# SiLU-gated product on one core: a 16-element transfer ahead of the first load, and a first store in one piece instead of three

## The chip, the core and the metric

The kernel runs on one core of a Trainium2 chip. Five engines of the core matter by name: ScalarE (ACT) and VectorE (DVE) compute, SyncE (SP) and ScalarE issue the DMA transfers, GpSimd (POOL) fills four constant tiles at the start; TensorE has no work. Sixteen DMA engines move the data between HBM and the on-chip memory SBUF, which has 128 partitions. Loads are issued by SyncE and go through DMA queue q1; stores are issued by ScalarE and go through q10. The metric is the device time of one execution in microseconds; smaller is better.

## The reference

The input has 32 x 512 = 16384 rows of 2048 float32. Each row is split in two halves of 1024; the output row is silu(first half) times second half.

```python
x = np.random.randn(32, 512, 2048).astype(np.float32)
half_dim = x.shape[-1] // 2
x1, x2 = x[..., :half_dim], x[..., half_dim:]
silu_x1 = x1 * (1 / (1 + np.exp(-x1)))
return (silu_x1 * x2).astype(np.float32)
```

So 134.22 MB are read and 67.11 MB written, and each element takes one activation or one multiply.

## The kernel before, in words

The rows are cut into 16 tiles of 1024 rows: 128 partitions with K = 8 rows each. Two tiles lie one after the other in each partition's share of memory (`view`, with RUN = 2). For each partition a load reads 8 x 2048 float32, 64 KB in one run, and a store writes 8 x 1024 float32, 32 KB in one run. There are two input buffers `xt` and two output buffers `ot`, used in turn.

For each tile, ACT applies Silu in place to the first half of `xt` (line 96), DVE multiplies it by the second half into `ot` (line 102), SyncE issues the load of the tile after the next into the buffer that has just been used up, and ACT's queue issues the store. Every transfer goes through `move` (line 77), so all of them have that line in the profile. SyncE's queue holds the sixteen loads alone; ACT's queue holds activations and stores in the order of the program, which is written out by hand (`manual_schedule`).

Tile 0 is computed in four chunks of 2 rows per partition (FIRST), tile 15 in chunks of 2, 3 and 3 rows (LAST); all others in one piece. Tile 15 is stored in three pieces too, each as soon as its chunk is multiplied. Tile 0 is stored, after its last chunk, in three pieces by partition (OPENING): partitions 0, 4, 8, ... (32 of them); partitions 2, 6, 10, ... (32); and the 64 odd ones. With 16 DMA engines these give 2, 2 and 4 partitions per engine.

Transfers take their completion semaphores from a set of eight, in turn, in the order in which they are recorded; `after` fixes that order between a tile's load and store, which of the two goes first changing every four tiles (`load_first`). `implied` declares waits that another wait already includes, and `settle_all_but` lets SyncE see all earlier transfers land before the last.

Of the kernel before, what the change touches and what calls it, by code (L numbers as in the profile page):

```python
# [1 line left out]

# [4 lines left out]


@with_exitstack
def kernel(  # L10
    ctx: ExitStack,
    tc: tile.TileContext,
    x: bass.AP,
    out: bass.AP,
):


    nc = tc.nc
    P = nc.NUM_PARTITIONS

    x_flat = x.flatten_outer_dims()
    out_flat = out.flatten_outer_dims()
    num_rows, in_cols = x_flat.shape
    half = in_cols // 2
    dt = x_flat.dtype

    K = 8
    FIRST = [2] * (K // 2)
    LAST = [2, 3, 3]
    OPENING = [  # L30
        (slice(0, None, 4), slice(None)),
        (slice(2, None, 4), slice(None)),
        (slice(1, None, 2), slice(None)),
    ]
    RUN = 2
    n_tiles = num_rows // (P * K)

    pool = ctx.enter_context(tc.tile_pool(name="pool", bufs=1))
    xts = [pool.tile([P, K, in_cols], dt, name=f"xt{b}") for b in range(2)]
    ots = [pool.tile([P, K, half], dt, name=f"ot{b}") for b in range(2)]  # L40

    def view(flat, i):
        return flat.rearrange("(g p t k) d -> g t p k d", p=P, t=RUN, k=K)[i // RUN, i % RUN]

    ctx.enter_context(tc.manual_schedule(engines={mybir.EngineType.Activation, mybir.EngineType.DVE}))

    sent = []
    loads, stores, silus, muls = {}, {}, {}, {}

    def implied(later, earlier, reason):  # L50
        for x in later:
            for y in earlier:
                tc.declare_no_dep(x, y, reason=reason)

    def earlier(done, i):
        return [ins for j in range(i % 2, i, 2) for ins in done[j]]

    def after(later, first):
        tc.add_manual_dep(
            later,  # L60
            first.name,
            mybir.DependencyInfo(mybir.DependencyClass.NoSync, mybir.DependencyReason.DATA),
            reason="order in which the transfers take their semaphores",
        )

    def settle_all_but(n, others):
        rest = nc.sync.nop(nofuse=True)
        for ins in sent[:-n] + others:
            tc.add_manual_dep(
                rest.ins,  # L70
                ins.name,
                mybir.DependencyInfo(mybir.DependencyClass.Sync, mybir.DependencyReason.DATA),
                reason="sync sees each earlier transfer land before the last ones",
            )

    def move(queue, out, in_):
        ins = queue.dma_start(out=out, in_=in_).ins  # L77
        sent.append(ins)
        return ins

    def load(i):
        loads[i] = [move(nc.sync, xts[i % 2][:], view(x_flat, i))]
        if i >= 2:
            implied(loads[i], earlier(loads, i), "the multiplies that this load awaits came after those loads")
            implied(loads[i], earlier(silus, i), "the multiplies that this load awaits came after those activations")

    def parts(sizes):
        assert sum(sizes) == K
        return [slice(sum(sizes[:n]), sum(sizes[:n + 1])) for n in range(len(sizes))]

    def compute(i, ot, chunks):
        xt = xts[i % 2]
        silus[i], muls[i] = [], []
        for ks in chunks:
            silus[i].append(
                nc.scalar.activation(  # L96
                    out=xt[:, ks, :half],
                    in_=xt[:, ks, :half],
                    func=mybir.ActivationFunctionType.Silu,
                ).ins  # L100
            )
            muls[i].append(nc.vector.tensor_mul(out=ot[:, ks], in0=xt[:, ks, :half], in1=xt[:, ks, half:]).ins)  # L102
        implied(muls[i], loads[i], "each multiply awaits an activation that came after the load")
        if i >= 2:
            implied(silus[i], earlier(silus, i), "the load that this activation awaits came after those activations")
            implied(silus[i], earlier(muls, i), "the load that this activation awaits came after those multiplies")
            implied(muls[i], earlier(muls, i), "the store that this multiply awaits came after those multiplies")

    def store(i, ot, pieces):
        ov = view(out_flat, i)  # L110
        stores[i] = [move(nc.scalar, ov[ps, ks], ot[ps, ks]) for ps, ks in pieces]

    ALL = slice(None)
    load(0)
    load(1)
    for i in range(n_tiles):
        ot = ots[i % 2]
        last = i == n_tiles - 1
        compute(i, ot, parts(FIRST if i == 0 else LAST if last else [K]))
        pieces = [(ALL, ALL)]  # L120
        if i == 0:
            pieces = OPENING
        elif last:
            pieces = [(ALL, ks) for ks in parts(LAST)]
        load_first = i // 4 % 2
        if load_first and i + 2 < n_tiles:
            load(i + 2)
        store(i, ot, pieces)
        if load_first and i + 2 < n_tiles:
            after(stores[i][0], loads[i + 2][0])  # L130
        if not load_first and i + 2 < n_tiles:
            load(i + 2)
            after(loads[i + 2][0], stores[i][-1])
    settle_all_but(1, muls[n_tiles - 1])


# [1 line left out]
_INS = ['x']  # L138
_OUTS = [((32, 512, 1024), 'float32')]


# [23 lines left out]
```

## Time and profile before

| | us |
|---|---|
| median of 3 runs (470.85 to 471.16) | 471.05 |
| span of the profiled execution | 469.2 |
| DVE busy | 139.5 |
| ACT busy | 114.2 |
| q1 (loads), share of 16 DMA engines' span | 66.4% |
| q10 (stores), share of 16 DMA engines' span | 33.2% |
| one silu of a whole tile, 128x8192 | 7.03 |
| one multiply of a whole tile, 128x8192 | 8.69 |

The span runs from the first to the last instruction of the profiled execution; the time of a run has some 1.9 us around it. A page's "busy" leaves out instructions that only issue a DMA; those stand in the timeline as SPq and ACTq, with the time that the issuing took. "To landing" is the time from the issue of a transfer to its completion, waiting in the queue included. The trace also keeps a record of every single DMA packet: queue, start, duration and bytes. Here a packet is one partition's run (64 KB of a load, 32 KB of a store, 8 or 12 KB of the last store's pieces) or the 4-byte update of a semaphore with which each DMA engine ends its share of a transfer. A record does not name its DMA engine, but a packet begins within a few ns of the end of the one before it on the same engine, so the sixteen sequences can be told apart by their phase.

### The profile page before, as it was taken

How to read it: one execution, taken by the hardware profiler on the slowest of the kernel's cores; microseconds unless marked ns; L12 is line 12 of the kernel's file. 1: busy time of each engine (PE TensorE's matmuls, PEld its weight loads, DVE VectorE, ACT ScalarE, POOL GpSimd, SP SyncE). 2: the span in 40 equal slices, each digit the busy share in tenths (PEclk: the TensorE clock that was granted, in tenths of full speed). 3: DMA queues.
4: the chain of work that ended last, by engine and by line, in shares of the span. 5: the costliest groups of instructions: out<-in, count | busy, mean ns of one | idle time of the engine just before them, and what ended most of it. 6: DMA issues, size and time to landing. Idle time of an engine off the chain costs nothing.

```text
span 469.2 us, 156 instructions
## 1 busy us (share of the span) xinstructions
DVE 139.5 (30%) x21; ACT 114.2 (24%) x22; POOL 0.2 (0%) x4
## 2 busy tenths in 40 slices
DVE  0070522407034070330704307042070520605152
ACT  1051405032050410504105050050501405014060
POOL 0000000000000000000000000000000000000000
DMA  8999999999999999999999999999999999999998
GB/s 358 447 447 374 475 402 433 416 492 402 411 439 486 408 402 447 475 419 402 444 439 458 402 436 413 492 402 416 433 486 408 402 447 475 419 402 444 450 402 358
DMA packets 4928, 201.33 MB, mean 429 GB/s; under 512 B 576, under 2 KB 576, under 8 KB 576
## 3 DMA queue, kind: packets, MB, share of 16 engines
q1 hardware_dynamic: 2304, 134.22, 66.4%
q10 hardware_dynamic: 2624, 67.11, 33.2%
HBM read 134.22 MB, written 67.11 MB: 429 GB/s over the span
## 4 chain that ended last, share of the span: by engine, by line
DMA 72%; DVE 14%; ACT 11%; DVEq 1%; issue 0%; SPq 0%
DMA xt<-in_x_dram 72%; DVE ot L102 14%; ACT xt L96 11%; DVEq L160 1%; SPq L77 0%
## 5 line engine op out<-in xcount | busy, mean ns | idle before, releaser
L102 DVE TENSOR_TENSOR ot<-xt 128x8192 f32<-128x8192 f32 (+2 forms) x21 | 139.5, 6659 | 320.8 <-ACT xt L96 320.8
L96 ACT ACTIVATE xt<-xt 128x8192 f32<-128x8192 f32 (+2 forms) x21 | 112.9, 5400 | 341.4 <-DMA xt<-in_x_dram 341.4
L96 ACT ACT_TABLE_LOAD x1 | 1.3, 1283 | 0.7 <-PEq L149 0.7
L149 POOL MEMSET const-bfloat16-1.0<- 128x1 bf16 x1 | 0.1, 102 | 0.0
L149 POOL MEMSET const-uint8-127<- 128x1 uint8 x1 | 0.1, 102 | 0.0
L149 POOL MEMSET const-float32-0.0<- 128x1 f32 x1 | 0.1, 99 | 0.2 <-issue 0.2
L149 POOL MEMSET const-float32-1.0<- 128x1 f32 x1 | 0.1, 99 | 0.0
## 6 DMA issues: line engine op xcount, KB each, us to landing
out_dram<-ot ACTq DMA_DIRECT2D x14, 4096.0 KB, 42.0
out_dram<-ot ACTq DMA_DIRECT2D x3, 1024.0 KB, 12.0
out_dram<-ot ACTq DMA_DIRECT2D x2, 1536.0 KB, 7.9
out_dram<-ot ACTq DMA_DIRECT2D x1, 2048.0 KB, 37.2
xt<-in_x_dram SPq DMA_DIRECT2D x16, 42.2
```

The source lines that it names most:

```text
L96: nc.scalar.activation(out=xt[:, ks, :half], in_=xt[:, ks, :half], func=mybir.ActivationFunctionType.Silu,).ins
L102: muls[i].append(nc.vector.tensor_mul(out=ot[:, ks], in0=xt[:, ks, :half], in1=xt[:, ks, half:]).ins)
L149: nc = _bacc.Bacc("TRN2", target_bir_lowering=False, num_devices=1)
L160: with _tile.TileContext(nc) as tc:
```

## The change

Ahead of load 0, SyncE issues a transfer that writes sixteen float32 zeros, from a constant tile that GpSimd fills at the start, to sixteen places in HBM: the first element of the last of the 8 rows of every eighth partition, in the output of tile 15. The store of tile 15 writes the right values there later. With sixteen elements on sixteen partitions, each DMA engine moves one. Load 0 comes after it in the order in which the transfers take their semaphores; it has no wait on it.

OPENING becomes one piece, so tile 0 is stored by one transfer of 128 partitions, like tiles 1 to 14.

```diff
     OPENING = [
-        (slice(0, None, 4), slice(None)),
-        (slice(2, None, 4), slice(None)),
-        (slice(1, None, 2), slice(None)),
+        (slice(None), slice(None)),
     ]
...
     ALL = slice(None)
+    with nc.allow_non_contiguous_dma(reason="one element on each DMA engine, ahead of the first load"):
+        first = move(nc.sync, view(out_flat, n_tiles - 1)[::8, K - 1, :1], nc.const_aps.tensor(0.0, [16, 1], dt))
     load(0)
+    after(loads[0][0], first)
     load(1)
```

## Prediction

> **What bounds the kernel now.** I read the busy time by slice first, then the DMA queues, the chain, the windows at both ends, and last the trace's single DMA packet records.
>
> From the page, the busy slices and the queues:
>
> ```profile
> DMA  8999999999999999999999999999999999999998
> DMA packets 4928, 201.33 MB, mean 429 GB/s; under 512 B 576, under 2 KB 576, under 8 KB 576
> q1 hardware_dynamic: 2304, 134.22, 66.4%
> q10 hardware_dynamic: 2624, 67.11, 33.2%
> ```
>
> q1 carries SyncE's loads, q10 ScalarE's stores. Together their packets fill 99.6% of 16 engines' span, so nothing that DVE or ACT does matters unless it leaves an engine without work. The waits say the same from the other side: ACT waits for loads and nothing else.
>
> ```profile
> ACT xt L96 <- DMA xt<-in_x_dram: 341.4, 16, 22.1
> DVE ot L102 <- ACT xt L96: 320.8, 17, 24.6
> ```
>
> The chain and the timeline, at both ends (start us, duration us, what):
>
> ```profile
> 0.73 0.37 SPq L77
> 1.10 0.05 issue
> 1.15 44.20 DMA xt<-in_x_dram
> ...
> 33.53 1.86 ACTq L77 DMA_DIRECT2D out_dram<-ot  x3
> ...
> 453.35 0.34 ACTq L77 DMA_DIRECT2D out_dram<-ot  x1
> ...
> 457.07 3.60 ACTq L77 DMA_DIRECT2D out_dram<-ot  x2
> ```
>
> The first load is issued at 0.73, and its first packet starts at 1.734. The last packet ends at 468.042, the span at 469.187.
>
> The packet records (start, duration, bytes, queue) show what is lost. A 64 KB load packet takes 2.418 us and a 32 KB store packet 1.213 on every engine; consecutive packets leave no gap. A tile has 8 of each per engine, about 29.0 us. Only two groups are longer. The 16 packets that open load 0 take 2.94 to 3.45, mean 3.187: 0.77 over. And the 16 load packets that start at 36.1 to 36.8, each just before its engine's first store packet, take 3.16 to 3.47, mean 3.283: 0.86 over. After that no load packet is over 2.425. One engine starts at 2.425, the other fifteen at 1.734 to 1.963; that engine is also last at the end, 468.042 against 467.849 for the next.
>
> This engine around load 1's end (starts in us; sem is the 9 ns completion packet):
>
> ```
> 36.794 load 7, 3.368 long | 40.158 store 1 | 41.368 load 8 | 43.782 store 2
> 44.991 load sem | 44.997 store sem (first opening store) | 45.003 load 1 | 47.417 store 3
> ... 54.664 store sem (second) ... 71.578 store sem (third) | 71.584 load sem
> ```
>
> Each engine takes one packet from one queue, then one from the other, and a completion packet uses a turn like a data packet. From 71.58 on a load and a store end in adjacent turns; at the end 448.578 store sem, 448.584 load sem. So when the last load lands, all 8 packets of store 14 remain, 9.7 us of cover for the last computation.
>
> **The change, part by part.**
>
> *Added: the zero transfer, first on SyncE's queue.* It waits for nothing: the zero tile is a MEMSET of 0.23 us, ahead of the release at 0.65. Queued behind it are load 0 and then all of SP's loads. SP's issues take 0.33 to 0.43 us; loads 0 and 1 are issued 0.42 apart (0.731, 1.151). So load 0 is issued up to 0.42 later. No row shows a 16-element issue; the nearest are these (0.33 with the shortest) and ACT's small stores (0.54 and 0.62). Bounds: 0, if the 1.00 us from issue to first packet holds a start-up that the zero pays, and 0.67 (0.62 plus a 0.05 gap). On the path it is all or nothing: engines have no work before it. I take 0.3, below 0.42, because the last engine begins 0.46 after the fifteenth: if what holds it ends by itself, the others move and it does not, and then the end moves by 0.42 - 0.19 = 0.23. Its 16 data and 16 completion packets are one of each per engine; at the 9 ns of a completion packet that is 0.02.
>
> *What the zero might remove.* The 0.86 at 36 us is paid once. Either it belongs to an engine's first write to HBM, and then the zero pays it while load 0's first read is under way (0.77 over anyhow), or to the first use of q10, which stays cold. Bounds -0.86 and 0. The store packets that follow take 1.213, their ordinary time; it is the load packet before that is long, as if the engine turned to a queue that was not ready. Nearest to that row is 0, and I take 0.
>
> *Removed: two opening stores.* Two completion packets of 9 ns: -0.02. ACT's three issues (0.54, 0.62, 0.62; 1.86 with gaps) become one, near 0.36; this saves nothing, ACT then idles until 45.38.
>
> *Moved: the order of turns.* The three stores use 8 + 3 turns, one uses 8 + 1. After the turn at 44.99 the store queue goes on with data where it had a completion packet, and again at 54.66, so it is two packets ahead. Load 2 and every later load lands 2 x 1.21 = 2.4 us later, and the last load leaves 6 packets of store 14, 7.3 us, instead of 8. The total work is the same, so this counts only if store 15 comes late. Its pieces are issued at 453.35, 457.07 and 460.33; each moves to 2.4 later, while the engines reach them when they did. The second is closest: on the slow engine its first packet is due at 460.72, and its issue moves to 459.49, which leaves 1.23. Issue to first packet, from load 0: 1.00 to 1.23 on fifteen engines, 1.69 on the slow one. So 0 to 0.46 on the engine that ends last; earlier engines may starve for 0.36 (due 460.13, there 460.49), inside their lead of up to 0.59. A latency as long as the first store's upper bound (issued 33.53, its turn not before 36.14: 2.6) would cost 1.4. I take 0.1. The third piece has 464.38 - 462.75 = 1.63: enough.
>
> Had a queue been drained in blocks, turns would not matter. The Trainium skill (DMA: Bandwidth & Descriptors, Queues, rings and completion order) says that an engine drains a packet of about 9 to 17 descriptors from one ring before it switches. By that, if each 64 KB move is a descriptor, a tile's 8 + 1 would go in a block, the two-packet lead would vanish, and the sum below would be 0.3 rather than 0.4. The records show single moves alternating (40.158, 41.368, 43.782), so I keep the 0.1.
>
> *Semaphores.* Each transfer takes the next of eight, so the zero and the two missing stores shift them by one. Reuse is eight transfers back, four tiles or 116 us, against a landing time of 44.2 at most: 0. A multiply waits for the store two tiles back, which now lands earlier relative to its load: 0. Last, rows of the third piece overwrite the zeros, 450 us later: 0.
>
> Sum: 0.3 + 0.02 + 0 - 0.02 + 0.1 = **+0.4 us**. The profiled span of 469.19 becomes 469.6. The median of the runs shown, 471.05, is 1.86 above the span; with the same rest that gives **471.45**, written 471.4.
>
> **The rivals.** 0.2% is 0.94 us, about what a measurement of this kernel can tell from no change.
>
> *A, my forecast:* the load's issue moves back, the 36 us stall stays. 471.4, its own range 471.0 to 471.9. Chance 0.42.
>
> *B, the zero takes the first-write stall:* 0.4 - 0.86 = -0.46, 470.6. For: the stall comes with the first store and never again over 1920 store packets. Against: the store packets themselves are of ordinary length. Chance 0.29.
>
> *C, slower: the last store starves the engines.* Place: second piece of the last store. It decides once issue to first packet exceeds 1.23 us on the last engine, or once the store queue gains a third packet (cover 6.1; then 1.21 more of wait). Price about 1.0 beside A's 0.3: 472.4. For: the lead of two packets follows from the turns, and the margin is small. Against: fifteen of sixteen engines began load 0 within 1.23 of its issue. Chance 0.20.
>
> *D, both cold starts go:* B, the late engine is no longer late (-0.19), and the issue is hidden: -0.86 - 0.19 = -1.05, 470.0. Against: what hides the issue must be paid by the zero first. Chance 0.07.
>
> *E, the zero holds up each engine until its write is confirmed:* by rows, the last packet ends at 468.042 and SP acts on it at 468.401, 0.36; load 0 would start that much after the zero's packet, which is hidden behind the 0.42 of the issue; 471.5, joined to A in its effect, chance 0.02. The Trainium skill (the same page, Anatomy of one DMA) puts a fixed 2.0 us on a transfer of the GpSimd path, mostly the receipt, heaviest in HBM. By that, as an estimate, load 0 would start at 2.73 instead of 1.73, 472.05. Rows speak against a blocked engine: completion packets of stores take 9 ns and the next packet starts 6 ns later.
>
> **How the numbers follow.** 471.4 is A's. Faster by over 0.2% (under 470.11) is D, 0.07. Slower (over 471.99) is C, and a little of A's upper end for the 0.62 issue: 0.22. The rest, A, B and E: 0.71. The range takes in A, B and most of C: 470.3 to 472.5, leaving out D and the 1.4 us end of C.
>
> **What would show it.** In the profile after: load 0 issued near 1.15 (0.73 if wrong); its first packets near 2.1, or still 1.73; the load packets before the first store still near 3.28, or 2.42 (B); ACT's silu of tile 2 starting 2.4 us later than 72.15, beside the start's shift; and the packets around 460 us, gapless or with a pause before the second piece (C). I am wrong if the stall at 36 us goes, if the pause is over half a us, or if anything idles between 45 and 450 us.

## The result and the profile after

The changed kernel takes 471.32 us (median of 20 runs), the kernel before 470.90 us (20 runs beside them): 0.42 us more. The ratio is 1.0013, with a 95% interval of 1.0007 to 1.0019. It goes with the means of the runs, 471.57 and 470.91, which lie further apart than the medians (1.0009) because four of the changed kernel's runs were long. The interval excludes 1, but the change lies within the 0.2% that I took as the bound of what counts. The forecast was 471.4, from +0.4.

The page of the changed kernel, busy slices and queues (packets, MB, share of 16 engines' span), still shows engines that are never idle for long:

```profile
DMA  8999998999999999999989999999999999999898
DMA packets 4928, 201.33 MB, mean 429 GB/s; under 512 B 576, under 2 KB 576, under 8 KB 576
q1 hardware_dynamic: 2336, 134.22, 66.3%
q10 hardware_dynamic: 2592, 67.11, 33.2%
```

The total of 4928 packets is the same: 32 more on q1 (16 zeros and their completions), 32 fewer on q10 (two transfers' completions). The chain at the start (start us, duration us, what) shows what is new:

```profile
0.73 0.38 SPq L75
1.11 0.06 issue
1.17 0.41 SPq L75
1.57 0.05 issue
1.63 44.10 DMA xt<-in_x_dram
45.73 0.02 issue
45.75 7.04 ACT xt L94
```

The place at 0.73 that load 0 had is the zero's; load 0 is issued at 1.17 and load 1 at 1.63 instead of 1.15. In the packet records the zeros pass at 1.60 to 1.76, and load 0's first packets start at 2.21 to 2.77, before at 1.73 to 2.43.

The timeline of ACT shows the two packets by which the store queue is ahead. Tile 2, before (first line) and after:

```profile
72.15 7.03 ACT L96 ACTIVATE xt<-xt 128x8192 f32<-128x8192 f32 x1 [19.74 <-DMA xt<-in_x_dram]
74.91 7.03 ACT L94 ACTIVATE xt<-xt 128x8192 f32<-128x8192 f32 x1 [22.13 <-DMA xt<-in_x_dram]
```

and the last tile, before (first line) and after:

```profile
449.08 4.56 ACT L96 ACTIVATE xt<-xt 128x2048 f32<-128x2048 f32 x2 [21.91 <-DMA xt<-in_x_dram]
451.73 4.56 ACT L94 ACTIVATE xt<-xt 128x2048 f32<-128x2048 f32 x2 [21.82 <-DMA xt<-in_x_dram]
456.00 0.34 ACTq L75 DMA_DIRECT2D out_dram<-ot  x1
459.71 3.61 ACTq L75 DMA_DIRECT2D out_dram<-ot  x2
```

Tile 2's silu starts at 74.91, 2.76 later than before, of which 0.37 had been there at tile 1 (45.75 against 45.38); the last tile's starts 2.65 later. The second piece of the last store is issued at 459.715 and its first packets start at 460.569, 0.85 later. A few engines were waiting for it, none for as long as 0.1 us: the first of them ended the first piece at 460.49. Between 45 and 450 us the packets of every engine follow one another without a gap of 25 ns. The end moved less than the start: the last packet ends at 468.326, against 468.042, 0.28 later, while load 0 was issued 0.44 later.

The load packets that run just before the first store still take 3.00 to 3.30 us, 3.137 in the mean, against 2.418 for others. That is 0.15 less than in the profiled execution before (3.283), and about what the end gained on the start.

### The profile page after: what moved, and what is told of

Read it like the earlier page. It is cut to its first block, busy times and chain, and to the rows that moved or that the text cites. A ratio compares the mean times of both kernels' runs of the same rounds, so it can differ in the third digit from the quotient of the medians.

```text
span 469.5 us, 153 instructions
## 1 busy us (share of the span) xinstructions
DVE 139.5 (30%) x21; ACT 114.2 (24%) x22; POOL 0.2 (0%) x4
## 2 busy tenths in 40 slices
DMA packets 4928, 201.33 MB, mean 429 GB/s; under 512 B 576, under 2 KB 576, under 8 KB 576
## 4 chain that ended last, share of the span: by engine, by line
DMA 72%; DVE 14%; ACT 11%; DVEq 1%; SPq 0%; issue 0%
DMA xt<-in_x_dram 72%; DVE ot L100 14%; ACT xt L94 11%; DVEq L161 1%; SPq L75 0%
```

## The experiments

Each experiment is an edit of one of the two kernels, timed in five rounds beside the kernel before, whose median was 470.85 to 470.94.

### Which of the two parts costs

The zero alone, with the first store in three pieces as before:

```diff
 (the kernel before)
+    with nc.allow_non_contiguous_dma(...):
+        first = move(nc.sync, view(out_flat, n_tiles - 1)[::8, K - 1, :1], nc.const_aps.tensor(0.0, [16, 1], dt))
     load(0)
+    after(loads[0][0], first)
```

> The zero transfer on SyncE's queue, with tile 0 still stored in three pieces. Theory 1 (the zero moves load 0's issue back, and that is the whole cost): the load's issue at 1.17 instead of 0.73, the time of the kernel before plus 0.2 to 0.45 us, about 471.3, with no runs near 472.5, since the last load leaves all 8 packets of store 14. Theory 2 (the time is lost at the end, where one store leaves only 6 packets): the time of the kernel before, 470.9 plus or minus 0.1.

Measured: 471.39 beside 470.85, ratio 1.0014 (1.0005 to 1.0023), a little above theory 1's span. Load 0 was issued at 1.18. One of its 11 runs was at 472.06, which the expectation had not allowed.

The one store alone:

```diff
     OPENING = [
-        (slice(0, None, 4), slice(None)),
-        (slice(2, None, 4), slice(None)),
-        (slice(1, None, 2), slice(None)),
+        (slice(None), slice(None)),
     ]
```

> Tile 0 stored in one piece, no zero transfer. Theory 1: 470.9 to 471.0 in most runs; loads from tile 2 on land 2.4 us later than in the kernel before. If the runs near 472.5 that the changed kernel has (4 of 20) come from a starved end, they are here too, about one in five near 472.1. Theory 2: 471.3, like the changed kernel. The load packet before the first store still takes about 3.2 us.

Measured: 470.94 beside 470.85, ratio 1.0005 (0.9997 to 1.0014): no difference. Its timeline has the later load of tile 2 without the zero's shift (72.15 before):

```profile
74.49 7.03 ACT L94 ACTIVATE xt<-xt 128x8192 f32<-128x8192 f32 x1 [21.76 <-DMA xt<-in_x_dram]
```

So the zero costs what was measured in the medians, and two store packets ahead cost nothing that can be told. Two of its 11 runs were long, 471.73 and 472.05, and the profiled execution is the first of these. In its records one engine's load packet at 394.5 takes 2.95 instead of 2.42, the last load lands on that engine 0.86 after all others, and the other fifteen wait 0.4 to 0.9 us for the second piece. The windows around it (length, busy by engine, clock, DMA share, GB/s) show it, that kernel first:

```profile
460.00:461.00 1.00, 1.00 (x2) 0.00 (x0) 0.00 (x0) 1.00 0.38 156
461.00:462.00 1.00, 1.00 (x1) 0.00 (x0) 0.00 (x0) 1.00 1.10 463
```

and the changed kernel's ordinary execution:

```profile
460.00:461.00 1.00, 1.00 (x1) 0.00 (x0) 0.00 (x0) 1.00 0.94 397
461.00:462.00 1.00, 1.00 (x1) 0.00 (x0) 0.00 (x0) 1.00 1.16 492
```

Between 460 and 461 the first has 0.38 of the engines' time in packets that start there, the second 0.94. This is rival C's place, and in this execution it opened because one engine had fallen behind.

### Is it the issue, or the writes

The suspected cost doubled:

```diff
+        second = move(nc.sync, view(out_flat, n_tiles - 1)[1::8, K - 1, :1], nc.const_aps.tensor(0.0, [16, 1], dt))
...
+    after(second, first)
+    after(loads[0][0], second)
```

> Two zero transfers ahead of load 0 on SyncE's queue (the second to sixteen other places), tile 0 stored in three pieces. If the issue on SyncE is the cost: load 0 is issued near 1.62 and the time rises by the same amount once more over the run with one zero, to 471.8 to 471.9, about 0.9 to 1.0 over the kernel before. If the zero costs once (a start-up that it pays, or a hold of the engines by its write): no more than 471.5.

Measured: 471.84 beside 470.91, +0.93. Load 0 was issued at 1.63. One zero cost +0.54, two cost +0.93, which is 0.47 for each; two issues lie 0.45 us apart.

The same single zero, one place later in the queue:

```diff
     load(0)
+    with nc.allow_non_contiguous_dma(...):
+        first = move(nc.sync, view(out_flat, n_tiles - 1)[::8, K - 1, :1], nc.const_aps.tensor(0.0, [16, 1], dt))
+    after(first, loads[0][0])
     load(1)
+    after(loads[1][0], first)
```

> The zero transfer on SyncE's queue between load 0 and load 1 instead of ahead of load 0; tile 0 stored in three pieces. If what the zero costs is only that it moves load 0's issue: load 0 is issued at 0.73, the engines have load 0's packets until 22 us while load 1 is issued near 1.6, and the time is that of the kernel before, 470.8 to 471.0. If its writes hold the engines, or cost in any other way wherever they stand: 471.3 to 471.4, like the zero ahead of load 0.

Measured: 470.96 beside 470.94, ratio 1.0002 (0.9993 to 1.0011). SyncE's queue, with the zero ahead (first fence) and behind load 0 (second):

```profile
0.73 0.40 SPq L77 DMA_DIRECT2D out_dram<-const-float32-0.0  x1
1.18 0.89 SPq L77 DMA_DIRECT2D xt<-in_x_dram  x2
```

```profile
0.73 0.37 SPq L77 DMA_DIRECT2D xt<-in_x_dram  x1
1.16 0.42 SPq L77 DMA_DIRECT2D out_dram<-const-float32-0.0  x1
1.63 0.41 SPq L77 DMA_DIRECT2D xt<-in_x_dram  x1
```

The interval alone would still hold a cost of 0.45. But ten of the 11 runs lie between 470.80 and 471.02, and all 11 with the zero ahead lie at 471.24 or more. The packet records show it directly. One engine at the end of load 0 (start us, duration ns):

```
21.964 (9) load 0 sem | 21.970 (9) zero | 21.976 (9) zero's sem | 21.981 (2418) load 1
```

So the same transfer, with the same writes, takes 11 ns (21.970 to 21.981) of an engine that has load packets to work on. What it costs ahead of load 0 is load 0's place in the queue. These records also set aside rival E, a hold until the write is confirmed: the next load packet starts as soon as the zero's completion packet, of 9 ns, is through.

### What the stall before the first store is

The stall of 0.86 us was the only thing that the zero could have bought. Three ways of opening the way for the first store were tried. The zero on ScalarE's queue, the one that carries the stores:

```diff
-        first = move(nc.sync, view(out_flat, n_tiles - 1)[::8, K - 1, :1], nc.const_aps.tensor(0.0, [16, 1], dt))
+        first = move(nc.scalar, view(out_flat, n_tiles - 1)[::8, K - 1, :1], nc.const_aps.tensor(0.0, [16, 1], dt))
```

> The zero transfer is issued by ScalarE's queue at the start instead of SyncE's; tile 0 in three pieces as before. If the stall before the first store is the first use of the store queue on each engine: the load packets that start at 36 us take 2.42 to 2.44 instead of 3.28, load 0 is issued at 0.73, and the time falls by 0.6 to 0.86, to 470.0 to 470.3. If the stall comes with the first full-size store whatever went through the queue: still 3.2 to 3.3, and 470.8 to 471.0.

Measured: 470.91 beside 470.85; the load packets before the first store take 3.315 in the mean. And the other direction, a read of 16 elements on that queue:

```diff
+        first = move(nc.scalar, ots[0][:16, 0, :1], view(x_flat, n_tiles - 1)[::8, K - 1, :1])
```

> As the run with the zero on ScalarE's queue, but the 16 elements go the other way, from HBM into a place of the output buffer that tile 0 overwrites. If the first use of the queue is what costs: the packets at 36 us take 2.42 to 2.44, 470.0 to 470.3. If it takes a write to HBM through that queue: they stay at 3.2 to 3.3 and the time at 470.8 to 471.0.

Measured: 470.90 beside 470.85; 3.327. So it is neither an engine's first write to HBM nor the first use of the store queue. My prediction had named these two as the only choices; both fall.

Then a small store of every partition at the start, of 512 B and of 4 KB for each:

```diff
+    EARLY = 128        # 1024 in the second run
+    nc.gpsimd.memset(ots[1][:, K - 1, :EARLY], 0.0)
     load(0)
+    early = move(nc.scalar, view(out_flat, n_tiles - 1)[:, K - 1, :EARLY], ots[1][:, K - 1, :EARLY])
+    after(early, loads[0][0])
```

> The kernel before with a small store of all 128 partitions, 512 B each (zeros into rows that the last store overwrites), on ScalarE's queue right after load 0's issue. If a store that uses every partition and all 8 turns of an engine opens the way once for all: the load packets at 36 us fall to 2.44 and a longer one shows up during load 0 or is hidden in its start; 470.2 to 471.0. If each entry of a store into an empty queue costs the same: still 3.3 at 36 us, a second long packet near 4 to 8 us, 471.1 to 471.9.

> The same with 4 KB for each partition, 0.5 MB, which is 1.2 us of the engines' time for itself. Opened once for all: 3.3 at 36 us falls to 2.44, 471.2 to 472.1. Cost of each entry: 3.3 stays, a second long packet in load 0, 472.1 to 473.0. If this differs from the 512 B store by more than the 1.2 us, the size of the entering packets matters.

Measured: 471.23 beside 470.91 (ratio 1.0007, 0.9999 to 1.0016), and 472.31 beside 470.91 (1.0029, 1.0018 to 1.0041). At 36 us the long packets stay, 3.171 and 3.299 in the mean. But neither entry of a small store into the running load 0 has a long packet of its own: behind each engine's first load packet none of load 0's is over 2.45. So the way isn't opened once for all. The second case has the times right (471.23 and 472.31), but not the reason: the small stores' own entry shows no cost, and with 512 B it falls just behind load 0's first packet, where the start could hide one. An entry of 4 KB packets doesn't cost what one of 32 KB packets does. Between the two small stores the size makes no difference: their times differ by 1.08, no more than the bytes account for (1.2 by the expectation).

Last, a small packet directly ahead of the large ones:

```diff
     OPENING = [
-        (slice(0, None, 4), slice(None)),
+        (slice(0, None, 8), slice(7, 8)),
+        (slice(0, None, 8), slice(0, 7)),
+        (slice(4, None, 8), slice(None)),
         (slice(2, None, 4), slice(None)),
         (slice(1, None, 2), slice(None)),
     ]
```

> The kernel before with tile 0's store in five pieces: one 4 KB packet for each engine first, directly behind it the other 28 KB of the same partition, then 1, 2 and 4 partitions for each engine. If the entry costs because a full 32 KB packet meets an empty queue, and a small packet ahead of it takes that away: the load packets before it fall from 3.3 to about 2.45, and the time by 0.6 to 0.9, to 470.0 to 470.3. If the entry of a queue of large packets costs the same whatever goes first: 3.2 to 3.4 before or just behind the small packet, 470.8 to 471.1.

Measured: 471.14 beside 470.89, ratio 1.0004 (0.9995 to 1.0013). The long load packet stands where the expectation's second case put it, between the 4 KB and the 28 KB packet, 3.087 in the mean. One engine's records (start us, duration ns):

```
36.115 (2429) load 64 KB | 38.543 (159) store 4 KB | 38.696 (3204) load 64 KB | 41.896 store sem
41.902 load sem | 41.908 (1062) store 28 KB | 42.966 (2418) load 64 KB
```

### How far the order of turns reaches

One more completion packet on the load queue while stores run:

```diff
 (the kernel with one store alone)
+        halves = [slice(0, None, 2), slice(1, None, 2)] if i == 2 else [slice(None)]
-        loads[i] = [move(nc.sync, xts[i % 2][:], view(x_flat, i))]
+        loads[i] = [move(nc.sync, xts[i % 2][ps], view(x_flat, i)[ps]) for ps in halves]
```

> No zero, tile 0 stored in one piece, and the load of tile 2 issued as two transfers of 64 partitions (every other one), which gives the load queue one more completion packet while stores run. Rule of turns: the store queue is three packets ahead from tile 2 on, the last load lands 1.2 us later than with the one store alone and leaves 5 packets of store 14; all engines then wait 0.9 to 1.3 us ahead of the second piece of the last store, and the time is 471.9 to 472.2. If the order of turns doesn't reach the end: 470.9 to 471.0.

Measured: 474.56 beside 470.91, ratio 1.0079 (1.0065 to 1.0093). The direction was right, the size three times too small. The last tile's timeline, and the windows ahead of its first and second pieces' packets:

```profile
455.78 4.56 ACT L95 ACTIVATE xt<-xt 128x2048 f32<-128x2048 f32 x2 [21.98 <-DMA xt<-in_x_dram]
460.04 0.34 ACTq L75 DMA_DIRECT2D out_dram<-ot  x1
463.76 3.61 ACTq L75 DMA_DIRECT2D out_dram<-ot  x2
```

```profile
459.50:460.80 1.30, 0.94 (x2) 1.30 (x2) 0.00 (x0) 1.00 0.06 25
463.50:464.60 1.10, 1.10 (x2) 0.00 (x0) 0.00 (x0) 1.00 0.02 7
```

The first piece is issued at 460.04 and starts at 460.88, the second at 463.76 and 464.60, and ahead of each the engines stand empty. What I had missed happens at 61 us. On every engine the last data packet of store 0 starts at 60.16 to 60.86, while store 1 is issued only at 61.45. The store queue runs out of data, and the sixteen load packets that start at 64.26 to 65.69, each ahead of its engine's first packet of store 1, are long again: 3.425 in the mean. The load queue runs dry at the same place: the second half of load 2 completes at 60.15 to 60.86, and load 3 is issued only at 61.45. Most of the last packets of store 0 take longer than 1.213, up to 1.864, and seven of the load packets behind them take 2.60 to 3.06. The engines also leave this place in different order; the last load ends at 451.8 to 453.0 on fifteen of them and at 455.4 on one, and ACT waits for that one. In the kernel with one store alone, the last packets of store 0 start at 62.56 to 63.15 with store 1 issued at 61.48, and no load packet there is over 2.43. From the issue of store 1 to the last packets of store 0 that is 1.1 us; in the changed kernel it is 1.36 (61.53 to 62.89). This is the margin by which the store queue does not run dry there.

This is the second sight of the stall, and it shows that the stall isn't tied to the first store ever. It fits a store of full-size packets that meets a queue with no data left. But here both queues were filled anew, so this run doesn't show the store's entry alone. Why the load packet ahead of it becomes long isn't settled by these runs.

### The runs at 472.4 to 472.6

Four of the changed kernel's 20 runs lay at 472.39 to 472.56, 1.1 to 1.2 above the median, and none of the 20 of the kernel before was over 471.16. I took them for starved ends and tried the end in four chunks, beside the changed kernel again:

```diff
 (the changed kernel)
-    LAST = [2, 3, 3]
+    LAST = [2, 2, 2, 2]
```

> The changed kernel with tile 15 computed and stored in chunks of 2, 2, 2 and 2 rows instead of 2, 3 and 3. The second piece is issued about 1.1 us earlier, near 458.5, well before the engines are done with the first. If the changed kernel's runs near 472.5 come from engines that wait for the second piece when one engine's last load lands late: none of the runs is over 472.0, the median is 471.2 to 471.35, and the profile has no wait ahead of the last pieces. If those runs have another cause: one in five stays near 472.5.

> The changed kernel once more, on the same chip as the run with four chunks, to compare their spread: a median of 471.3, and some of the runs near 472.4, 1.0 to 1.2 above the median. If its runs above 472 were chance of that chip: all within 471.2 to 471.8.

Measured: 471.37 and 471.43 beside 470.89. With four chunks one of 11 runs was at 472.22; the changed kernel itself had none over 471.73 this time, which at a rate of 4 in 20 happens by chance about once in twelve. The pieces are issued at 456.20, 458.40, 460.60 and 462.81, no engine waits, and the median is no better. The kernel with the zero behind load 0, whose store is in three pieces, had one run at 472.17 of 11. So such runs come without the short end too, and the theory that all of them are starved ends isn't borne out. Two profiles are of long runs. That of the one store alone (471.73) is a starved end behind an engine that fell behind, as shown above. That of the zero alone is its slowest run (472.06), and there no engine waits at the end: fourteen engines end by 468.16, the last two at 468.80 and 469.13. The lag stems from the opening. The last engine's completion packet comes 0.67 us after the eighth of the sixteen at the end of load 0, 1.00 at load 1, 1.15 at load 2, and still 1.12 at the last load. Why an engine falls behind, and whether that makes the changed kernel's long runs too, of which no profile was taken, stays open.

## Why the prediction was right

**The sum: right, in part by luck.** +0.4 was forecast, +0.42 measured (20 runs); +0.54 when it was compared again (11 runs). The zero's term of 0.3 was about 0.15 too small, and the 0.1 for the end was not seen as a difference in the one store alone; the two errors nearly cancel. The means, which count the long runs, lie 0.66 apart.

**The zero ahead of load 0: direction and mechanism right, size too small.** I took 0.3, between 0 and 0.67, because the one late engine might not move. The latest first packet did move, from 2.425 to 2.767, and the earliest from 1.734 to 2.214. One late engine is no fixed feature of this start either: with load 0 issued at 0.73, the latest first packet starts at 2.03 in the store in five pieces and at 2.62 with the early store of 4 KB. From load 0's issue to its first packet it is 1.05 with the zero ahead, 1.00 before, so the zero pays no start-up either. The zero alone cost 0.54, two cost 0.93, and one behind load 0 cost 0.02. The right term is the distance of two issues on SyncE, 0.44 here (0.731 to 1.168), with nothing taken off. One reading was wrong without effect: the MEMSET of the zero tile starts at 0.23 and takes 0.10, still ahead of 0.65.

**What the zero might remove: 0, right, with a wrong list of causes.** The stall stayed (3.137 against 3.283), and B and D fell with it. Over all profiles but that of the five-piece store it lies between 3.14 and 3.47, so 3.137 is the low end of a spread and no gain that can be told.

**The order of turns: right.** Two packets ahead, loads 2.3 to 2.4 later, as the one store alone shows (74.49 against 72.15). By the rule of the Trainium skill (DMA: Bandwidth & Descriptors, Queues, rings and completion order) that an engine drains a packet of about 9 to 17 descriptors of one ring before it switches, and if each 64 KB move is a descriptor, the number of opening transfers would not have moved tile 2; here it did, and the records show one move of each queue in turn.

**The end: 0.1, right in effect.** I had allowed 1.00 to 1.23 us from issue to first packet, from load 0's start. At the last store it was 0.84 to 0.85 in three kernels (the changed one, the one store alone, load 2 in two), so the margin on the last engine was wider than I made it, and C did not come in the median. It came in one long run, that of the one store alone at 471.73. The run with load 2 in two shows that C is real one step further on, and dearer than the 1.0 that I priced, since both queues also run dry in mid-kernel.

**Semaphores, the completion packets, the single issue of the first store: 0.** Nothing in the one store alone, which has the last two, contradicts it.

## What to carry to other kernels

Ahead of the first large load, a DMA issue on the same queue cost its whole issue time here, though it moved only 16 elements: 0.45 us, and nothing that can be told one place later. When all DMA engines are full, look for terms only at the two ends and at places where a queue runs empty. Where two queues alternate packet by packet, as here, the number of transfers sets which queue is ahead; it cost nothing until one ran dry, so compute how many packets of cover are left before splitting or joining transfers.

## What I had not expected

- A store of 32 KB packets (28 KB in one run) that entered a queue without data made the load packet ahead of it longer by 0.7 to 1.05 us in the mean of the sixteen engines. A store of 4 KB packets or less, entering the running load 0, made none over 2.45 us behind the first.
- 16 elements of 4 bytes cost SyncE 0.38 to 0.42 us to issue, as much as a load of 8 MB (0.33 to 0.43).
- Splitting one load of sixteen in two cost 3.65 us.
